# A two-layer hybrid decoder trunk: the last scaling as three tasks a row tile, four weight loads in halves, warm-up products on a constant

## The chip, the core and the metric

The kernel runs on one core of a Trainium2 chip. The metric is the device time of one execution in microseconds (us). All tensors in memory are float32. Five engines take part, each with its own instruction stream: TensorE (PE in the profile, with PEld for its weight loads), VectorE (DVE), ScalarE (ACT), GpSimd (POOL) and SyncE (SP), which issues nearly all transfers.

## What is computed

Each of two layers takes the residual stream x (256 rows of 1024), norms it, projects it to 3584 columns, lets three groups of heads attend, gates each group's output with a silu, and projects the 1024 gated columns back into x. A final norm with its own gain follows. Shortened:

```python
def reference(x, mem, norm_g, w_in, mem_norm_g, w_mem_kv, w_out, final_norm_g):
    for layer in range(2):
        h = rms_norm(x, norm_g[layer])
        proj = h @ w_in[layer]                     # 1024 -> 3584
        sb_q, sb_k, sb_v, sb_g, mb_q, mb_k, mb_v, mb_g, mem_q, mem_g = split(proj)
        o_sb = stick_breaking_attention(sb_q, sb_k, sb_v) * silu(sb_g)     # 6 heads of 64
        o_mb = moba_attention(rotary(mb_q), rotary(mb_k), mb_v) * silu(mb_g)  # 6 heads
        mk, mv = split(rms_norm(mem, mem_norm_g[layer]) @ w_mem_kv[layer])
        o_mem = memory_attention(mem_q, mk, mv) * silu(mem_g)              # 4 heads
        x = x + concat([o_sb, o_mb, o_mem]) @ w_out[layer]
    return rms_norm(x, final_norm_g)
```

## The kernel before, in words

**Order.** The program is recorded by a small scheduler (`Sched`). Tasks are Python generators; each yields the engine that it wants next and the names that must be ready, and the scheduler, with a cost for every operation, picks the task that can start first. What it picks is the fixed order of instructions on each engine. The costs do not run on the chip; there only the order and the semaphores count.

**Precision.** Every weight chunk `raw` comes by a transfer, is rounded to a high part by a cast (`hi_task`, the CAST `hl<-raw`, L290 on ACT or L311 on DVE) and gets a low part by a subtraction on DVE (`lo_task`, TENSOR_TENSOR `hl<-raw,hl`, L296). The activations have a high and a low part too, in `T`, and a product takes three terms. All products are recorded by the helper `mm` (L273).

**Weights.** The two layers' weights are cut into 107 chunks of 192 to 768 KB, in the order in which PE uses them (`chunks`). They share one ring of memory, `raw`: `dma_room` issues chunk j on SP once the scheduler has seen the low parts of all the chunks that lay in its place. `dma_chunk` issues one transfer a chunk (helper `dma`, L378). SP is one queue in program order, so a load that waits there holds up every later one. On the same queue go the attention weights' trips through memory: DVE transposes 32 by 32 blocks into `D`, SP stores `D` to `Z` (L1005) and loads it back rearranged into `T` or `F` (L1018, four loads a trip). PE then multiplies these by the values (`bank<-T,mv`, `bank<-T,mb_v`, `bank<-F,sb_v`).

Of the chunks that the change touches, chunk 38 is the last of the projection to sb_v in layer 0, chunk 52 the second of `w_out` in layer 0 (512 KB), chunk 68 the last of mb_k in layer 1 (192 KB), chunk 78 the first of sb_k in layer 1. Chunks 38 and 78 have 384 KB.

**Start.** `main` first fills a tile `junk` with zeros on DVE (L1131) and multiplies it with itself 14 times on PE (seven products of 512 columns, seven of 128), whose results nobody reads. The first real products are those of chunk 0 with the first 128 rows of the transposed x, which ACT and DVE scale into `T`.

**End.** In layer 1 the output projection gives, for each row tile t of 128 rows, the sums of two or three blocks of columns: 512 and 512 for t = 0, and 512, 256 and 256 for t = 1, of which the last starts from x in the accumulator. `resid_task` adds the block to x on DVE and squares it on ACT with a running sum. `gain_task` multiplies by the final gain `gb` on DVE. When the last block of a row tile is squared, `out_task` makes the reciprocal root with two small ACT instructions, scales the row tile by it in three pieces (columns 640 to 1023 on ACT, 0 to 255 and 256 to 639 on DVE) and stores each piece. In this version the three pieces are steps of one generator: the piece on ACT comes first and the next one is asked for only when it is recorded.

Of the kernel before, what the change touches and what calls it, by code (L numbers as in the profile page):

```python
# [9 lines left out]
BF = mybir.dt.bfloat16  # L10
# [6 lines left out]
D = 1024  # L17
# [45 lines left out]
ML_W = 0.0  # L63
ML_T = 300.0
ML_S = 200.0
MEM_AT = 0
ORDER = (["sb_qk", "mb_k", "mem_q", "mb_q", "mk", "mb_v", "mv", "sb_v", "sb_g", "mb_g", "mem_g"], ["mk",
         "mb_k", "mb_q", "mem_q", "sb_q", "sb_k", "mv", "mb_v", "mem_g", "mb_g", "sb_v", "sb_g"])
# [45 lines left out]
class Sched:  # L114
# [37 lines left out]
    def _avail(self, k, eng):  # L152
        r = k.req
        t = k.t
        if k.eng == eng:
            t += 0.0 if eng == "pe" else LAT_SAME
        elif k.eng:
            t += LAT_CROSS
        for n in r.get("need", ()):
            if n not in self.ready:  # L160
                return None
            t = max(t, self.ready[n])
        for tag in r.get("alloc", ()):
            items = self.res[tag].items
            spare = r.get("spare", 0)
            if callable(spare):
                spare = spare()
            if "form" in r and r["form"] == self.form:
                spare = r.get("spare2", spare)
            if len(items) <= spare:  # L170
                return None
            t = max(t, self.res[tag].best()[0])
        cond = r.get("cond")
        if cond is not None and not cond():
            return None
        return t + r.get("late", PE_LATE) if eng == "pe" and k.gen.__name__ != "main" else t
# [60 lines left out]
def hybrid_trunk(ctx: ExitStack, tc: tile.TileContext, x, mem, norm_g, w_in, w_mem_kv, w_out,  # L237
                 final_norm_g, xT, memT, gcols, consts, out):
    nc = tc.nc
# [234 lines left out]
    def dma_chunk(now=0.0, q=None):  # L474
        j = prog["dma"]
        if j >= len(chunks):
            return
        p, kk, c, w = chunks[j]
        n = len(kk)
        dma(raws(j).rearrange("p (k c) -> p k c", c=w),  # L480
            p.src[:, kk[0]:kk[0] + n, c:c + w], ("raw", j), q, now)
        prog["dma"] += 1
        if j in X_AT:
            load_xT(X_AT[j], X_AT[j] + 1, now=now)
        for t, at in enumerate((X0_AT, X1_AT)):
            if j == at:
                dma(xs[:, t, :], x_r[:, t, :], ("x", t), now=now)
        if j == CST_AT:
            dma(cst, consts[:, 0:512], "cst", now=now)
            dma(S.res["w"].items[0][2][:, :256], consts[:, 512:768], "msk", now=now)  # L490
# [14 lines left out]
    def lo_task():  # L505
        for j, (p, kk, _, w) in enumerate(chunks):
# [1 line left out]
            tt(los(j), raws(j), his(j).bitcast(F32), OP.subtract)  # L508
            S.mark(("lo", j))
            prog["lo"] = j + 1  # L510
            dma_room(S.cur.t)

    def urgent(which):
        return lambda: -5 if prog[which] <= prog["cur"] + URG else 60
# [18 lines left out]
    load_xT(2, 3)  # L533
    dma_chunk()
    load_xT(3, 4)
    dma_room()

    def bcast_row(vec, name):
        nc.gpsimd.dma_start(gb, bass.AP(tensor=vec.tensor, offset=vec.offset, ap=[[0, 128], [1, D]]))
# [574 lines left out]
    def out_task(t, nb):  # L1114
        r = ss[1, t][:, 7:8]
        yield from rstd(ss[1, t], nb, r)
        edge = (0, 512, 768, 1024) if nb == 3 else (0, 512, 1024)
        for eng, a, b, q in (("act", 640, D, nc.scalar if t else nc.sync), ("dve", 0, 256, nc.sync), ("dve", 256, 640, nc.sync)):
            yield R(eng, need=[("gain", n, t) for n in range(nb) if edge[n] < b and edge[n + 1] > a])
            s = xs[:, t, a:b]  # L1120
            if eng == "act":
                act(s, s, AF.Copy, scale=r)
            else:
                ts(s, s, r)
            q.dma_start(out_r[:, t, a:b], s)


    def main():
        hT, mT = Ts
        yield R("dve")  # L1130
        nc.vector.memset(junk, 0.0)  # L1131
        S.op("dve", 150.0)
        _, (acc,) = yield R("pe", alloc=["bank"])
        for n in (512,) * 7 + (128,) * 7:
            mm(acc[:, :n], junk[:, :128], junk[:, :n], True, True)
        S.free("bank", acc)
        scale_task(uT, ("xT",), 0, hT, ("h", 0), P_H0)
        for t in range(2):
# [177 lines left out]
    S.spawn(setup(), 0)  # L1316
    S.spawn(hi_task(), urgent("hi"))
    S.spawn(lo_task(), urgent("lo"))
    S.spawn(main(), 100)
    S.run()  # L1320

# [44 lines left out]
```

## Time and profile before

| | |
|---|---|
| median of 3 runs | 265.92 us (265.19 to 267.18) |
| the profiled execution | 265.58 us, of which the span of instructions is 263.8 us |
| granted TensorE clock | 0.993 |
| PE busy | 256.1 us (97%), 1597 products |
| DVE, ACT busy | 225.0 us (85%), 190.2 us (72%) |
| transfers | 67.05 MB, 254 GB/s over the span |

The page has six parts: busy time by engine; the span in 40 slices; the transfer queues; the chain of work that ended last, followed back from the last instruction; the costliest groups of instructions; and the issues of transfers with the time to their landing. The trace can also be asked for a timeline (start and duration in us, engine, line, operation, output and inputs, how many were merged, and in brackets how long the engine sat idle before it and what released it), for the table of waits (who waited for what: total, times, longest), and for the busy shares in chosen stretches. The products' ends are modelled and overlap the next product's start, so PE's busy share says little by itself; what PE waited for says more.

### The profile page before, as it was taken

How to read it: one execution, taken by the hardware profiler on the slowest of the kernel's cores; microseconds unless marked ns; L12 is line 12 of the kernel's file. 1: busy time of each engine (PE TensorE's matmuls, PEld its weight loads, DVE VectorE, ACT ScalarE, POOL GpSimd, SP SyncE). 2: the span in 40 equal slices, each digit the busy share in tenths (PEclk: the TensorE clock that was granted, in tenths of full speed). 3: DMA queues.
4: the chain of work that ended last, by engine and by line, in shares of the span. 5: the costliest groups of instructions: out<-in, count | busy, mean ns of one | idle time of the engine just before them, and what ended most of it. 6: DMA issues, size and time to landing. Idle time of an engine off the chain costs nothing.

```text
span 263.8 us, 4793 instructions
## 1 busy us (share of the span) xinstructions
PE 256.1 (97%) x1597; PEld 227.6 (86%) x1597; DVE 225.0 (85%) x517; ACT 190.2 (72%) x393; POOL 6.1 (2%) x18
## 2 busy tenths in 40 slices
PE   8999999999999999999999999999999999999990
PEld 5889999998899987878899998888898899787880
DVE  3878999999899999989799586999999995978353
ACT  4789995999698795967665272966897899356133
POOL 1002000000100000000000000000000000000000
PEclk9999999999999999999999999999999999999997
DMA  7999998989979999978955939599878996961004
GB/s 202 359 395 357 390 361 264 317 295 283 373 209 315 314 299 253 267 244 274 308 172 201 352 95 243 212 264 320 263 211 216 330 279 229 254 233 53 0 0 159
DMA packets 49880, 67.05 MB, mean 254 GB/s; under 512 B 4224, under 2 KB 41472, under 8 KB 49856
## 3 DMA queue, kind: packets, MB, share of 16 engines
q1 hardware_dynamic: 48912, 64.85, 77.4%
q0 software_dynamic: 512, 1.31, 1.7%
q10 hardware_dynamic: 432, 0.59, 0.7%
q8 instruction: 12, 0.20, 0.4%
q14 instruction: 12, 0.10, 0.1%
HBM read 57.29 MB, written 9.44 MB: 253 GB/s over the span
## 4 chain that ended last, share of the span: by engine, by line
PE 87%; DMA 7%; ACT 1%; SPq 1%; DVE 1%; issue 0%; DVEq 0%; ACTq 0%
PE bank L273 86%; DMA T<-Z 3%; DMA raw<-in_w_out_dram 3%; DMA raw<-in_w_in_dram 2%; PE bank L279 1%; SPq L1018 1%; ACT hl L290 1%; ACT junk L292 1%; DVE xs L296 1%; SPq L378 0%; DVE xs L304 0%; ACT ss L292 0%; DVE T L300 0%; DVEq L1362 0%; DVE ss L628 0%
## 5 line engine op out<-in xcount | busy, mean ns | idle before, releaser
L296 DVE TENSOR_TENSOR hl<-raw,hl 128x768 fp32r<-128x768 f32 (+5 forms) x107 | 99.6, 947 | 7.9 <-ACT hl L290 6.0
L273 PE MATMUL bank<-T,hl 128*128 128x256 f32 (+1 forms) x646 | 106.1, 322 | 0.2 <-DVE T L300 0.2
L273 PEld LDWEIGHTS bank<-T,hl 128*128 128x128 f32 x646 | 92.6, 189 | 11.7 <-issue 1.8
L290 ACT CAST hl<-raw 128x768 fp32r<-128x768 f32 (+5 forms) x105 | 85.3, 841 | 17.0 <-DMA raw<-in_w_in_dram 6.4
L273 PE MATMUL bank<-hl,T 128*128 128x384 f32 (+1 forms) x448 | 79.6, 335 | 0.0
L273 PEld LDWEIGHTS bank<-hl,T 128*128 128x128 f32 x448 | 76.5, 188 | 2.2 <-issue 0.3
L273 PE MATMUL bank<-hl,mxhi 128*128 128x512 f32 (+1 forms) x144 | 41.2, 367 | 0.0
L273 PEld LDWEIGHTS bank<-hl,mxhi 128*128 128x128 f32 x144 | 26.1, 189 | 4.9 <-issue 0.4
L273 PE MATMUL bank<-hl,mxlo 128*128 128x512 f32 (+1 forms) x72 | 26.3, 366 | 0.0
L877 DVE STREAM_TRANSPOSE D<-w 128x384 f32<-128x384 f32 (+1 forms) x32 | 19.2, 602 | 3.2 <-ACT w L292 2.9
L292 ACT ACTIVATE junk<-xs 128x512 bf16<-128x512 f32 (+1 forms) x12 | 7.3, 610 | 13.6 <-DVE xs L296 13.1
L273 PEld LDWEIGHTS bank<-hl,mxlo 128*128 128x128 f32 x72 | 13.6, 189 | 2.2
L292 ACT ACTIVATE T<-uT,gc 128x256 fp32r<-128x256 f32 x24 | 11.4, 506 | 2.7 <-DMA uT<-xT_dram 2.7
L810 DVE TENSOR_TENSOR_SCAN a<-a,a 128x256 f32<-128x256 f32 (+1 forms) x24 | 12.8, 539 | 0.1
L292 ACT ACTIVATE a<-bank 128x384 f32<-128x384 f32 x24 | 11.3, 483 | 1.6 <-DVE a L810 0.9
L292 ACT ACTIVATE w<-w,st 128x128 f32<-128x128 f32 (+1 forms) x24 | 10.7, 448 | 2.3 <-DVE st L830 2.2
L292 ACT ACTIVATE a<-a 128x384 f32<-128x384 f32 x24 | 11.8, 522 | 0.2
L300 DVE SCALAR_TENSOR_TENSOR T<-uT,gc,T 128x256 fp32r<-128x256 f32 x24 | 11.4, 476 | 0.6 <-ACT T L292 0.6
L304 DVE TENSOR_SCALAR w<-w,st 128x256 f32<-128x256 f32 (+1 forms) x40 | 11.2, 323 | 0.2
L296 DVE TENSOR_TENSOR xs<-bank,xs 128x512 f32<-128x512 f32 (+1 forms) x8 | 5.3, 656 | 6.6 <-PE bank L273 6.5
L292 ACT ACTIVATE w<-bank,st 128x256 f32<-128x256 f32 x16 | 7.4, 488 | 4.1 <-DVE st L843 4.1
L290 ACT COPY gT<-bank 128x256 f32<-128x256 f32 x10 | 3.6, 372 | 7.7 <-PE bank L273 7.7
(106 smaller groups left out, 218.6 us busy)
## 6 DMA issues: line engine op xcount, KB each, us to landing
raw<-in_w_in_dram SPq DMA_DIRECT2D x39, 384.0 KB, 4.8
Z<-D SPq DMA_DIRECT2D x16, 384.0 KB, 5.0
raw<-in_w_out_dram SPq DMA_DIRECT2D x8, 512.0 KB, 6.0
raw<-in_w_in_dram SPq DMA_DIRECT2D x18, 192.0 KB, 4.0
raw<-in_w_in_dram SPq DMA_DIRECT2D x6, 576.0 KB, 5.7
raw<-in_w_in_dram SPq DMA_DIRECT2D x13, 256.0 KB, 4.9
raw<-in_w_mem_kv_dram SPq DMA_DIRECT2D x6, 512.0 KB, 6.2
raw<-in_w_out_dram SPq DMA_DIRECT2D x4, 768.0 KB, 6.4
```

The costliest lines, as they stand in the source:

```text
L273: nc.tensor.matmul(out, lhsT=lhsT, rhs=rhs, start=start, stop=stop, **kw)
L279: nc.tensor.transpose(out, in_, idt)
L290: nc.scalar.copy(out, in_)
L292: nc.scalar.activation(out, in_, func, **kw)
L296: nc.vector.tensor_tensor(out, a, b, op=op)
L300: nc.vector.scalar_tensor_tensor(out, a, s, b, op0=op0, op1=op1)
L304: nc.vector.tensor_scalar(out, a, s, None, op0=op)
L810: nc.vector.tensor_tensor_scan(a[:, r0:r1], a[:, r0:r1], u[:, r0:r1], 0.0, OP.add, OP.add)
L877: nc.vector.transpose(o, w[:, :n * 128].rearrange("p (m j r) -> p m j r", j=4, r=32))
L1018: nc.sync.dma_start(Fv[32 * j:32 * j + 32, i0:i1], Zv.rearrange("(i r) (j e) -> j r i e", i=4, j=4)[j, :, i0:i1])
```

## The change

Four edits:

- `out_task` now makes the reciprocal root, marks it ready, and starts three tasks of a new function, `store_task`, one for each piece. The pieces of a row tile can now be recorded in any order, each with its own store. The last piece of t = 1 on ACT still goes out on ACT's own queue, all others on SP.
- `dma_chunk` splits the transfer of the chunks in `SPLIT` (38, 52, 68, 78) in two: by rows of the weight where the chunk has several blocks of 128 rows, by columns for chunk 68, which has one. The cast of a split chunk is still one instruction, so it needs both halves.
- The 14 first products multiply a constant of ones that the preamble writes on POOL before any engine starts, read with a step of zero, in place of `junk`. The filling of `junk` goes; it stays as the place that the squares are written to.
- A task that would issue loads one by one (`load_task`, with `after` in the scheduler) is written down but not started, since `LOADS` is 20.

```diff
--- before.py
+++ after.py
@@ -63,6 +63,9 @@
 ML_W = 0.0
 ML_T = 300.0
 ML_S = 200.0
+SPLIT = (38, 52, 68, 78)
+LOADS = 20
+P_LD = 50
 MEM_AT = 0
 ORDER = (["sb_qk", "mb_k", "mem_q", "mb_q", "mk", "mb_v", "mv", "sb_v", "sb_g", "mb_g", "mem_g"], ["mk",
          "mb_k", "mb_q", "mem_q", "sb_q", "sb_k", "mv", "mb_v", "mem_g", "mb_g", "sb_v", "sb_g"])
@@ -156,7 +159,7 @@
             t += 0.0 if eng == "pe" else LAT_SAME
         elif k.eng:
             t += LAT_CROSS
-        for n in r.get("need", ()):
+        for n in (*r.get("need", ()), *r.get("after", ())):
             if n not in self.ready:
                 return None
             t = max(t, self.ready[n])
@@ -477,8 +480,13 @@
             return
         p, kk, c, w = chunks[j]
         n = len(kk)
-        dma(raws(j).rearrange("p (k c) -> p k c", c=w),
-            p.src[:, kk[0]:kk[0] + n, c:c + w], ("raw", j), q, now)
+        dst, src = raws(j).rearrange("p (k c) -> p k c", c=w), p.src[:, kk[0]:kk[0] + n, c:c + w]
+        if j in SPLIT:
+            m = n // 2
+            one, two = ((slice(0, m), slice(0, w)), (slice(m, n), slice(0, w))) if m else ((slice(0, 1), slice(0, w // 2)), (slice(0, 1), slice(w // 2, w)))
+            dma(dst[:, one[0], one[1]], src[:, one[0], one[1]], None, q, now)
+            dst, src = dst[:, two[0], two[1]], src[:, two[0], two[1]]
+        dma(dst, src, ("raw", j), q, now)
         prog["dma"] += 1
         if j in X_AT:
             load_xT(X_AT[j], X_AT[j] + 1, now=now)
@@ -508,7 +516,15 @@
             tt(los(j), raws(j), his(j).bitcast(F32), OP.subtract)
             S.mark(("lo", j))
             prog["lo"] = j + 1
-            dma_room(S.cur.t)
+            if LOADS >= 20:
+                dma_room(S.cur.t)
+
+    def load_task():
+        while prog["dma"] < len(chunks):
+            j = prog["dma"]
+            yield R("sp", need=[("lo", max(rawp[j][1]))] if rawp[j][1] else [],
+                    after=[("raw", j - LOADS)] if j >= LOADS else [])
+            dma_chunk(S.cur.t)
 
     def urgent(which):
         return lambda: -5 if prog[which] <= prog["cur"] + URG else 60
@@ -533,7 +549,8 @@
     load_xT(2, 3)
     dma_chunk()
     load_xT(3, 4)
-    dma_room()
+    if LOADS >= 20:
+        dma_room()
 
     def bcast_row(vec, name):
         nc.gpsimd.dma_start(gb, bass.AP(tensor=vec.tensor, offset=vec.offset, ap=[[0, 128], [1, D]]))
@@ -1114,25 +1131,28 @@
     def out_task(t, nb):
         r = ss[1, t][:, 7:8]
         yield from rstd(ss[1, t], nb, r)
+        S.mark(("rstd", t))
+        for eng, a, b in (("dve", 0, 256), ("dve", 256, 640), ("act", 640, D)):
+            S.spawn(store_task(t, nb, r, eng, a, b), a // 256)
+
+    def store_task(t, nb, r, eng, a, b):
         edge = (0, 512, 768, 1024) if nb == 3 else (0, 512, 1024)
-        for eng, a, b, q in (("act", 640, D, nc.scalar if t else nc.sync), ("dve", 0, 256, nc.sync), ("dve", 256, 640, nc.sync)):
-            yield R(eng, need=[("gain", n, t) for n in range(nb) if edge[n] < b and edge[n + 1] > a])
-            s = xs[:, t, a:b]
-            if eng == "act":
-                act(s, s, AF.Copy, scale=r)
-            else:
-                ts(s, s, r)
-            q.dma_start(out_r[:, t, a:b], s)
+        yield R(eng, need=[("rstd", t)] + [("gain", n, t) for n in range(nb) if edge[n] < b and edge[n + 1] > a])
+        s = xs[:, t, a:b]
+        if eng == "act":
+            act(s, s, AF.Copy, scale=r)
+        else:
+            ts(s, s, r)
+        (nc.scalar if t and eng == "act" else nc.sync).dma_start(out_r[:, t, a:b], s)
 
 
     def main():
         hT, mT = Ts
         yield R("dve")
-        nc.vector.memset(junk, 0.0)
         S.op("dve", 150.0)
         _, (acc,) = yield R("pe", alloc=["bank"])
         for n in (512,) * 7 + (128,) * 7:
-            mm(acc[:, :n], junk[:, :128], junk[:, :n], True, True)
+            mm(acc[:, :n], nc.const_aps.tensor(1.0, [128, 128], BF), nc.const_aps.tensor(1.0, [128, n], BF), True, True)
         S.free("bank", acc)
         scale_task(uT, ("xT",), 0, hT, ("h", 0), P_H0)
         for t in range(2):
@@ -1316,6 +1336,8 @@
     S.spawn(setup(), 0)
     S.spawn(hi_task(), urgent("hi"))
     S.spawn(lo_task(), urgent("lo"))
+    if LOADS < 20:
+        S.spawn(load_task(), P_LD)
     S.spawn(main(), 100)
     S.run()
 
```

On PE and ACT the program has the same instructions in the same order, apart from the operands of the 14 first products. On DVE the filling of `junk` is gone and the end is in another order. The end of DVE's stream before, where `xs` is the row tiles, `ss10` and `ss11` hold the sums and the reciprocal roots of t = 0 and t = 1, and TENSOR_SCALAR on `xs` is a piece of the last scaling:

```order
L296 TENSOR_TENSOR xs_64<-bank7_97,xs_64 128x256
L296 TENSOR_TENSOR xs_64<-xs_64,gb_71 128x512
L628 TENSOR_SCALAR ss11_135<-ss11_135 128x1
L296 TENSOR_TENSOR xs_64<-xs_64,gb_71 128x256
L304 TENSOR_SCALAR xs_64<-xs_64,ss10_134 128x256
L296 TENSOR_TENSOR xs_64<-bank4_94,gb_71 128x256
L304 TENSOR_SCALAR xs_64<-xs_64,ss10_134 128x384
L304 TENSOR_SCALAR xs_64<-xs_64,ss11_135 128x256
L304 TENSOR_SCALAR xs_64<-xs_64,ss11_135 128x384
```

And now:

```order
L299 TENSOR_TENSOR xs_64<-bank7_97,xs_64 128x256
L299 TENSOR_TENSOR xs_64<-xs_64,gb_71 128x512
L307 TENSOR_SCALAR xs_64<-xs_64,ss10_134 128x256
L307 TENSOR_SCALAR xs_64<-xs_64,ss10_134 128x384
L645 TENSOR_SCALAR ss11_135<-ss11_135 128x1
L299 TENSOR_TENSOR xs_64<-xs_64,gb_71 128x256
L299 TENSOR_TENSOR xs_64<-bank4_94,gb_71 128x256
L307 TENSOR_SCALAR xs_64<-xs_64,ss11_135 128x256
L307 TENSOR_SCALAR xs_64<-xs_64,ss11_135 128x384
```

Both pieces of t = 0 moved ahead of three operations of t = 1. On SP the five stores stood in the order 384 (ACT's piece), 256 and 384 of t = 0, 256 and 384 of t = 1, and stand now as 256, 384 and 384 (ACT's piece) of t = 0, then 256 and 384 of t = 1.

SP's stream around chunk 52, before (`T1`, `F1` are the places of attention weights, `Z` their place in memory, `raw` from `in_w_out` are chunks 51, 52, and one row further on 53):

```order
L378 DMA raw_88<-in_w_in_dram 128x2x256
L378 DMA raw_88<-in_w_out_dram 128x2x512 x2
L1018 DMA T1_74<-Z1_112 32x4x192 x4
L1005 DMA Z0_111<-D0_107 128x768
L1018 DMA T1_74<-Z2_113 32x4x192 x4
L378 DMA raw_88<-in_w_out_dram 128x2x512
L1005 DMA Z1_112<-D1_108 128x768
L1018 DMA F1_106<-Z0_111 32x4x192 x4
```

And now:

```order
L381 DMA raw_88<-in_w_in_dram 128x2x256
L381 DMA raw_88<-in_w_out_dram 128x2x512
L381 DMA raw_88<-in_w_out_dram 128x512 x2
L1035 DMA T1_74<-Z1_112 32x4x192 x4
L1022 DMA Z0_111<-D0_107 128x768
L381 DMA raw_88<-in_w_out_dram 128x2x512
L1035 DMA T1_74<-Z2_113 32x4x192 x4
L1022 DMA Z1_112<-D1_108 128x768
L1035 DMA F1_106<-Z0_111 32x4x192 x4
```

Chunk 52 is two rows of one block each, and chunk 53's load moved ahead of the four loads from `Z2`. At the other three split chunks one more row stands and nothing else moved.

## The prediction

> **What bounds the kernel now.** I read the table of waits of PE first, because its busy share of 97% rests on modelled ends.
>
> ```profile
> PE bank L273 <- DVE junk L1131: 1.2, 1, 1.2
> PE bank L273 <- DMA T<-Z: 0.3, 1, 0.3
> PE bank L273 <- DVE T L300: 0.2, 1, 0.2
> ```
>
> These are all the waits of PE: 1.7 us in three places, none for a weight chunk (`hl`). The same table for PE's own weight loads, which overlap its products, has one short one:
>
> ```profile
> PEld bank L273 <- DVE hl L296: 0.2, 1, 0.2
> ```
>
> So PE does not stand still for a cast, a low part or a load of weights. The chain of waits tells the same and gives the places.
>
> ```profile
> 2.12 4.43 DMA raw<-in_w_in_dram
> ...
> 7.38 88.75 PE bank L273 x593
> ...
> 98.08 6.77 DMA raw<-in_w_out_dram
> ...
> 106.69 7.95 DMA T<-Z
> ...
> 140.16 114.79 PE bank L273 x696
> ```
>
> So there are three parts: a head to 7.38 us, set by the arrival of a weight load; a body in which PE computes without a break but for the 0.3 us near 114.7 (a load of attention weights, `T<-Z`, that went out at 106.69 and landed 7.95 later); and a tail from 254.95 to 263.8, 8.85 us, in which the last blocks are added, normed, scaled and stored. A change pays only in the head, in the tail, or by that one wait. The body is PE's own work, which the change leaves as it is.
>
> **The change part by part. Warm-up products on the constant.** The timeline of the first microseconds:
>
> ```profile
> 0.87 0.27 DVE L1131 MEMSET junk<- 128x256 uint32 x1 [0.87 <-PEq L1350]
> 1.19 3.37 PE L273 MATMUL bank<-junk 128*128 128x512 bf16 x14 [1.19 <-DVE junk L1131]
> 4.01 0.51 ACT L292 ACTIVATE T<-uT,gc 128x256 fp32r<-128x256 f32 x1 [1.99 <-DMA uT<-xT_dram]
> 4.57 2.58 PE L273 MATMUL bank<-T,hl 128*128 128x256 f32 x18
> ```
>
> DVE, free after the preamble at 0.87, fills `junk` in 0.27, and PE starts at 1.19. Without that wait PE can start when DVE could, near 0.87: 0.32 earlier, and 0.27 of DVE go. Neither reaches the path: the first real products start at 4.57 when ACT's scaled block is there (4.01 + 0.51 = 4.52), which waits for a load of x, and the next after 7.15 wait again until 7.38 for DVE (the last row of PE's waits), behind the load of weights that ends at 2.12 + 4.43 = 6.55. The cover is thus 0.05 us at 4.57 and a load of weights at 7.38. I take 0. The bounds: below, a gain of 0.2, the wait at 7.38 if it were to go, which nothing here supports; above, the constant is read with a step of zero, an operand form that no product in this trace has. The 14 products take at most 3.37 now. They may end at 4.57 + 0.23 (what PE idles before 7.38) = 4.80 before they cost anything, so from 0.87 they may last 3.93, or 1.17 times as long. At twice the length they would end at 0.87 + 6.74 = 7.61, a loss of 2.8. I take the row itself (the same 14 products, same sizes) as the nearest, and keep the loss as a rival.
>
> **Halved loads.** What must be known is whether the cast of the chunk waits for its load. ACT's rows for chunks 38, 52 (with 53), 68 (with 66 and 67) and 78 (with 77 and 79):
>
> ```profile
> 58.88 0.83 ACT L290 CAST hl<-raw 128x768 fp32r<-128x768 f32 x1
> ...
> 96.16 2.00 ACT L290 CAST hl<-raw 128x1024 fp32r<-128x1024 f32 x2 [0.35 <-PE bank L273]
> ...
> 130.49 1.33 ACT L290 CAST hl<-raw 128x384 fp32r<-128x384 f32 x3
> ...
> 155.74 2.37 ACT L290 CAST hl<-raw 128x768 fp32r<-128x768 f32 x3
> ```
>
> Three have no idle time before them: ACT came from other work, and the chunk lay ready. The second idled 0.35, but for PE, which had to finish with the place in `hl`. A half that arrives sooner is therefore worth 0 at all four, even before one asks whether PE waits for the cast. What it costs is one more issue on SP each and whatever the queue loses by smaller transfers. From the page's issues:
>
> ```profile
> raw<-in_w_in_dram SPq DMA_DIRECT2D x39, 384.0 KB, 4.8
> raw<-in_w_in_dram SPq DMA_DIRECT2D x18, 192.0 KB, 4.0
> ```
>
> Half the bytes land 0.8 us sooner, not in half the time. If the halves follow each other without overlap, a split costs 2 × 4.0 − 4.8 = 3.2; if the second runs behind the first, it costs one issue. The timeline of SP around chunk 52 (the first row), and PE's row that uses the loads behind it:
>
> ```profile
> 85.92 0.37 SPq L378 DMA_DIRECT2D raw<-in_w_out_dram  x1
> 86.38 1.84 SPq L1018 DMA_DIRECT2D T<-Z  x4
> 88.32 0.38 SPq L1005 DMA_DIRECT2D Z<-D  x1
> 88.74 3.25 SPq L1018 DMA_DIRECT2D T<-Z  x4
> 92.10 0.39 SPq L378 DMA_DIRECT2D raw<-in_w_out_dram  x1
> ...
> 102.15 0.82 PE L273 MATMUL bank<-T,mb_v 128*64 128x256 f32 x8
> ```
>
> An issue is 1.84 / 4 = 0.46. The loads `T<-Z` at 88.74 now stand behind chunk 53's load, which stood at 92.10, so they may go up to 0.46 + 0.39 later, and land behind 512 KB more; PE uses them at 102.15, more than 10 us after the last went out. The load on which PE waits at 114.7 went out at 106.69, some 14 us behind these, and the chain goes back from it to a load of weights issued at 98.08, not to SP's queue between 86 and 92, so an issue more there is swallowed before. I take 0 for all four splits, with a loss of 3.2 and a gain of 0.3 (the wait at 114.7 gone, because chunk 53's load is out of the way sooner) as ends. The Trainium skill, "DMA: Bandwidth & Descriptors", section "Rules for kernel authors", speaks against this edit: many small transfers should be joined into one large one, and below 64 KB one pays mostly overhead. The halves here have 96 to 256 KB; by the rows above the overhead is there too (0.8 for half the bytes), and the sum by the rule would be a loss somewhere below 3.2, by the rows' cover 0.
>
> **The last scaling.** DVE's and ACT's timelines of the tail:
>
> ```profile
> 256.75 0.68 DVE L296 TENSOR_TENSOR xs<-xs,gb 128x512 f32<-128x512 f32 x1
> 257.48 0.21 DVE L628 TENSOR_SCALAR ss<-ss 128x1 f32<-128x1 f32 x1
> 257.61 0.42 DVE L296 TENSOR_TENSOR xs<-xs,gb 128x256 f32<-128x256 f32 x1
> 257.94 0.35 DVE L304 TENSOR_SCALAR xs<-xs,ss 128x256 f32<-128x256 f32 x1
> 258.54 0.42 DVE L296 TENSOR_TENSOR xs<-bank,gb 128x256 f32<-128x256 f32 x1 [0.25 <-ACT junk L292]
> 258.88 1.00 DVE L304 TENSOR_SCALAR xs<-xs,ss 128x384 f32<-128x384 f32 x3
> ```
>
> ```profile
> 256.52 0.53 ACT L292 ACTIVATE ss<-ss 128x1 f32<-128x1 f32 x2
> ...
> 257.52 0.62 ACT L292 ACTIVATE xs<-xs,ss 128x384 f32<-128x384 f32 x1
> ...
> 258.54 0.53 ACT L292 ACTIVATE ss<-ss 128x1 f32<-128x1 f32 x2
> 259.10 0.61 ACT L292 ACTIVATE xs<-xs,ss 128x384 f32<-128x384 f32 x1
> ```
>
> The root of t = 0 is there at 257.05. The pieces of t = 0 now follow the gain at 256.75, which hands over near 257.34 (an operation starts some 0.09 before the last one's end: 257.61 + 0.42 against 257.94). The 256 columns take until 257.69; the 384 start a third of the three-piece row's 1.00 later, at 257.67, and end near 258.05. Then comes the sum of t = 1 (257.61 − 257.48 = 0.13 until the next starts), at 258.0 in place of 257.48; ACT needs it at 258.54, so 0.3 of cover is left. Then the gain (257.94 − 257.61 = 0.33), done by 258.5. The next gain starts at 258.54 as before, since it waits for ACT, and ends at 258.96. The root of t = 1 is there at 259.07. Before, the 384 columns of t = 0 stood in between, and the last piece ended at 259.88. Now the last two start at 259.10 and, with two thirds of 1.00, end at 259.77: 0.1 sooner. The stores:
>
> ```profile
> 258.17 2.50 SPq L1125 DMA_DIRECT2D out_dram<-xs  x5
> ...
> 260.21 0.46 SPq L1125 DMA_DIRECT2D out_dram<-xs  x1
> ```
>
> ```profile
> 259.74 0.37 ACTq L1125 DMA_DIRECT2D out_dram<-xs  x1
> ```
>
> ```profile
> 259.00:260.00 1.00, 0.00 (x0) 0.00 (x0) 0.88 (x3) 0.68 (x2) 0.00 (x0) 0.93 0.93 326
> ...
> 261.00:262.00 1.00, 0.00 (x0) 0.00 (x0) 0.00 (x0) 0.00 (x0) 0.00 (x0) 0.50 0.99 357
> ```
>
> Five stores leave SP from 258.17 to 260.21; the last column of the stretches is GB/s and the one before it the queues' busy share. SP's issues are 0.46 apart when they queue, so the last store went out at 260.21, 0.33 after its piece was done, and the one before it at 259.75: SP had been held by the stores of t = 0, whose last piece came from DVE after 258.88. Now t = 0 goes out at 257.72 (its first piece), 258.18 and 258.64 (ACT's piece is done at 258.14), then SP is idle until the first piece of t = 1 is done at 259.10 + 0.35 = 259.45, and the last store leaves at 259.48 + 0.46 = 259.94: 0.27 sooner. The other end: the 1 MB moves at 326 to 357 GB/s without a gap from 259 on, so the finish may follow the bytes. Then the 0.5 MB of t = 0, out 0.45 sooner (257.72 for 258.17) and with no piece held back to 259, are clear before t = 1 comes, whose bytes no longer queue behind them; at most the whole 0.45 goes through to the end. Between 0.27 and 0.45 I take 0.4, nearer to the bytes, since the queues are 0.99 busy just before the end.
>
> **Sum.** 0 + 0 − 0.4 on the profiled execution: 265.58 − 0.40 = 265.18. The median of the runs shown lies 0.34 above that execution, which would make it 265.52. I forecast 265.3, between the two: 0.2% faster, far within the 1% that a measurement of this kernel can tell from no change.
>
> **Rivals.** (1) The stores are bound at the end by landing alone and the new order gains nothing: 265.6. For it: the last store's queue share of 0.99. Against it: its bytes wait behind others that now go sooner. (2) The wait at 114.7 goes too: 265.18 − 0.3 = 264.9. For it: chunk 53's load leaves up to 3.4 us earlier (88.74 for 92.10) and clears the queue. Against: the chain goes back to a load issued at 98.08, which waits for DVE. (3) Slower: the split of chunk 52 and the load moved behind it make the attention weights for the products near 114.7 late. PE already waits there, so every bit counts from the first. The price is between 0.46 (one issue) and 3.2 (a serial half); the middle, 1.8, gives 265.18 + 1.8 = 267.0, the end 268.4. Against it: 14 us lie between. (4) Slower: the products on the constant take longer, from 1.17 times on; at twice the time 265.18 + 2.8 = 268.0. For it: no row shows that form. Against it: only the address step differs.
>
> **How the numbers follow.** The forecast 0.60, rival 1 0.13, rival 2 0.12, rival 3 0.10, rival 4 0.05. Faster by over 1% would be below 263.3, and no case reaches it: 0.03 for what I do not see. Slower by over 1% is above 268.6: rival 4 from a little over twice the time on, or rival 3's end of 268.4 with the scatter of the runs, together 0.06. The rest, 0.91, is no change. The range: down to 264.3, which is rival 2 less the 0.7 by which the lowest run lies under the median, rounded in; up to 267.0, rival 3's middle, which also covers the highest run, 267.18, less the 0.4.
>
> **What would show it.** Right: PE's waits keep `T<-Z` and `T` and lose `junk`; the first products start near 0.9 and the real ones still at 4.6 and 7.4; SP's last store leaves 0.87 after the second root's end (259.07 here) in place of 1.14; ACT's casts of the four chunks have no idle time for a load. Wrong: a first group of products that lasts over 3.9 us, a wait of PE for `T<-Z` over 0.5, or a row of waits with `hl`.

## The result and the profile after

The changed kernel takes 264.96 us (median of 9 executions, 264.51 to 265.07), the kernel before, run beside it, 266.33 (9 executions, 265.19 to 267.18 without one of 286.4, which the ratio leaves out). The ratio is 0.9949, with a 95% interval from 0.9929 to 0.9968. The forecast was 265.3 and no change that can be told; the time lies in its range and under 1%, but the gain is 1.4 us by the medians, and 1.07 by the profiled executions (265.58 and 264.51), where 0.4 was worked out. So the question is where the rest came from.

The waits of PE in the changed kernel, its weight loads left out, are a single row, the one before its first product (PEq is PE's sequencer):

```profile
PE bank L276 <- PEq L1372: 0.8, 1, 0.8
```

Both waits that the forecast kept are gone, the 0.2 for `T` at 7.38 and the 0.3 for `T<-Z` near 114.7. The head in the timeline of PE:

```profile
0.78 3.89 PE L276 MATMUL bank<-const-bfloat16-1.0 128*128 128x512 bf16 x14 [0.78 <-PEq L1372]
4.65 4.58 PE L276 MATMUL bank<-T,hl 128*128 128x256 f32 x27
```

The products on the constant start 0.41 sooner than those on `junk`, take 3.89 in place of 3.37, and the real ones start at 4.65 and run on without a break. The tail on DVE and on ACT:

```profile
256.30 0.68 DVE L299 TENSOR_TENSOR xs<-xs,gb 128x512 f32<-128x512 f32 x1
256.90 0.68 DVE L307 TENSOR_SCALAR xs<-xs,ss 128x256 f32<-128x256 f32 x2
257.49 0.21 DVE L645 TENSOR_SCALAR ss<-ss 128x1 f32<-128x1 f32 x1
257.62 0.42 DVE L299 TENSOR_TENSOR xs<-xs,gb 128x256 f32<-128x256 f32 x1
258.08 0.42 DVE L299 TENSOR_TENSOR xs<-bank,gb 128x256 f32<-128x256 f32 x1
258.65 0.68 DVE L307 TENSOR_SCALAR xs<-xs,ss 128x256 f32<-128x256 f32 x2
```

```profile
258.08 0.53 ACT L295 ACTIVATE ss<-ss 128x1 f32<-128x1 f32 x2
258.65 0.61 ACT L295 ACTIVATE xs<-xs,ss 128x384 f32<-128x384 f32 x1
259.29 0.35 ACTq L1146 DMA_DIRECT2D out_dram<-xs  x1
```

Both pieces of t = 0 are now scaled right behind their gain, and the last row stands alone: both pieces of t = 1 follow its root at once. SP's stores run from 257.27, and its last one leaves at 259.45, 0.84 behind the root's end (258.08 + 0.53):

```profile
257.27 2.60 SPq L1146 DMA_DIRECT2D out_dram<-xs  x5
```

```profile
259.45 0.42 SPq L1146 DMA_DIRECT2D out_dram<-xs  x1
```

**Where the 1.07 lies.** I compared the two executions product by product. Both have the same 1597 products, and between two waits they keep step to about 0.03 us, so the difference changes only at a few places. The start of PE's products is 0.17 ahead after 7.4, 0.48 after 114.8, and 0.45 at the last one. The two steps stand where the kernel before waited, at 7.38 and near 114.7. From the start of the last product to the landing of the last store it was 5.14 and is 4.76 (0.38 less), and from that landing to the end of the span it was 1.13 and is 0.89 (0.24 less). In sum 1.08. The last of these was in no reckoning of mine. It is a list on SP. A semaphore is a counter that a transfer raises when it has landed; the program closes with eight checks, one for each semaphore that the transfers use, in a fixed order and some 0.06 us apart in the trace. The transfers take these eight semaphores in turn, so the number of transfers decides where in the list the last store stands. Before, four more checks came after the one that waited for it; with four transfers more, it is the last of the list.

### The profile page after: what moved, and what is told of

The parts are those of the page before. It is cut to its first block, busy times and chain, and to the rows that moved or that the text cites. A ratio compares the mean times of both kernels' runs of the same rounds, so it can differ in the third digit from the quotient of the medians.

```text
span 262.7 us, 4802 instructions
## 1 busy us (share of the span) xinstructions
PE 256.6 (98%) x1597; PEld 228.0 (87%) x1597; DVE 224.6 (85%) x516; ACT 189.9 (72%) x393; POOL 6.1 (2%) x18
## 3 DMA queue, kind: packets, MB, share of 16 engines
q0 software_dynamic: 512, 1.31, 1.8%
## 4 chain that ended last, share of the span: by engine, by line
PE 97%; ACT 1%; DVE 0%; issue 0%; DVEq 0%; ACTq 0%
PE bank L276 96%; PE bank L282 1%; ACT junk L295 1%; ACT ss L295 0%; DVE xs L299 0%; DVE xs L307 0%; ACT xs L295 0%; DVEq L1384 0%; ACTq L295 0%
```

## The experiments

Each was timed in five rounds, the kernel before run beside it on the same chip. The theory at the start (A) was a sum of three parts, each taken as the work of the change: 0.4 from the stores, 0.3 from the wait at 114.7, 0.25 from the list. The rivals laid the gain on one edit, or on chance. Of the first four, three each take one part of the change to the kernel before, and the fourth halves other chunks.

**w_only, the warm-up products alone.**

```diff
-        nc.vector.memset(junk, 0.0)
...
-            mm(acc[:, :n], junk[:, :128], junk[:, :n], True, True)
+            mm(acc[:, :n], nc.const_aps.tensor(1.0, [128, 128], BF), nc.const_aps.tensor(1.0, [128, n], BF), True, True)
```

> The kernel before with the constant warm-up products alone (no memset, nothing else moved). Theory A (the gain is a sum of three: about 0.4 from the stores, 0.3 from the wait for T<-Z near 114.7 that went, 0.25 from the list of semaphore checks that SP works off after the last landing): no change, within 0.3 of the kernel before; first product near 0.8, the first real one still at 4.6, and PE's wait for T<-Z near 114.7, the 4 checks after the last landing and the store order as before. Rival B (the warm-ups carry the rest, by an earlier start or a steadier clock at the head): 0.5 to 0.9 faster, with PE ahead of the kernel before by that much before 20 us, and runs that scatter less.

Measured: 265.74 us against 265.74, ratio 1.0001 (0.9984 to 1.0018). PE's waits:

```profile
PE bank L273 <- PEq L1349: 0.8, 1, 0.8
PE bank L273 <- ACT hl L290: 0.5, 1, 0.5
```

No change in time, as theory A and the forecast have it, and the runs scatter as before (265.35 to 267.25): rival B falls. But theory A wanted the wait for `T<-Z` to be there, and it is not. Nothing that this kernel edits comes near 114.7. The row behind the first, a wait for a cast that ends at 9.9 us, is new.

**s_only, the last scaling alone.**

```diff
-        for eng, a, b, q in (("act", 640, D, nc.scalar if t else nc.sync), ("dve", 0, 256, nc.sync), ("dve", 256, 640, nc.sync)):
...
+        for eng, a, b in (("dve", 0, 256), ("dve", 256, 640), ("act", 640, D)):
+            S.spawn(store_task(t, nb, r, eng, a, b), a // 256)
```

> The kernel before with the last scaling in three tasks alone. Theory A: 0.4 faster, all of it behind PE's end: the last store leaves SP 2.1 after PE's end in place of 2.4 and lands 0.4 sooner counted from PE's end; 4 checks stand behind the last landing as before, so landing to end stays 1.13. Rival C (the stores carry everything, 1.1 to 1.4): 1.1 or more faster. Rival D (the landing of the bytes alone decides): 0 to 0.1 faster.

Measured: 265.35 us against 265.74, ratio 0.9988 (0.9965 to 1.0012). The interval holds no change too, but the profile is clear: from the last product to the last landing 4.78 us (5.14 before), from there to the end 1.13, as before. That is theory A's 0.4, and it rules out C, and D's 0 to 0.1 too. In this execution too PE waited for nothing but its start:

```profile
PE bank L273 <- DVE junk L1135: 1.2, 1, 1.2
```

**h_only, the four halved loads alone.**

```diff
+SPLIT = (38, 52, 68, 78)
...
+        if j in SPLIT:
...
+            dma(dst[:, one[0], one[1]], src[:, one[0], one[1]], None, q, now)
+            dst, src = dst[:, two[0], two[1]], src[:, two[0], two[1]]
+        dma(dst, src, ("raw", j), q, now)
```

> The kernel before with the four splits alone, chunk 53's load moved up with them. Theory A: 0.55 faster: 0.3 from PE's wait for T<-Z near 114.7 that is gone, and 0.25 behind the last landing, because four more transfers put the last store's semaphore at the end of SP's closing list (0 checks after it in place of 4; landing to end 0.87 in place of 1.13). Rival E (the wait near 114.7 is chance of one execution): 0.25 faster, with the wait there in some profiles and not in others. Rival F (neither; halves cost nothing and bring nothing, as predicted): within 0.1 of the kernel before.

Measured: 265.51 us against 265.74, ratio 0.9986 (0.9968 to 1.0005): 0.23, which is rival E's number by the medians; the interval holds A's 0.55 too, and no change. From the last product to the last landing 5.12, as before; from there to the end 0.90. No wait near 114.7. The head of this execution shows one source of the scatter:

```profile
1.19 3.91 PE L274 MATMUL bank<-junk 128*128 128x512 bf16 x14 [1.19 <-DVE junk L1137]
4.86 4.35 PE L274 MATMUL bank<-T,hl 128*128 128x256 f32 x23
```

The stretches of a microsecond on PE, with the products begun in each (x), here and then in s_only:

```profile
5.00:6.00 1.00, 1.00 (x6) 1.00 0.70 225
6.00:7.00 1.00, 1.00 (x7) 1.00 0.94 297
```

```profile
5.00:6.00 1.00, 1.00 (x6) 1.00 0.86 253
6.00:7.00 1.00, 1.00 (x11) 1.00 0.97 368
```

Products of 256 columns go at half rate (213 ns each) until 7.1 us in h_only and until 5.9 in s_only, and at 120 ns after; the column before the queues' share, the granted clock, reads 1.00 in all four rows. At 8.4 us h_only is 0.56 behind s_only, and it is 0.56 behind at its last product. The end of the half rate came between 3.9 us (the kernel before) and 7.1 over the profiles, whatever the kernel. The Trainium skill, "TensorE: Matmul & The Clock Gate", section "What's actually happening", tells of a free-running activity window of 3.4 us, so that the moment of full speed moves with where in it the first product falls, by 0.5 either way. A moment that moves fits; by these profiles it moves by 3.2 us.

**l4, four other chunks halved.** They were chosen so that no instruction and no load changes its place among the others; SP only issues four transfers more. The edit is h_only's with other numbers.

```diff
-SPLIT = (38, 52, 68, 78)
+SPLIT = (45, 48, 87, 90)
```

> The kernel before with four other chunks split (45, 48, 87, 90), so that no load or instruction changes its place among the others: SP only issues 4 transfers more. Theory A: 0.25 faster, all of it after the last landing (0 checks after it in place of 4; landing to end 0.87 in place of 1.13), with PE's wait for T<-Z near 114.7 as before (0.2 to 0.4). Rival E (that wait is chance): 0.25, and the wait may be gone. Rival F (the closing list costs nothing, the splits neither): within 0.1 of the kernel before.

Measured: 265.42 us against 265.74, ratio 0.9982 (0.9963 to 1.0000): 0.32. From the last landing to the end 0.89. So four halves of other chunks bring the same 0.24. PE has another wait in this execution, for `F<-Z` (0.2), and falls behind by another 0.5 near 108.

After these four, the wait at 114.7 was struck from the theory: two kernels that do not touch that place do not have it. What stayed is A': 0.37 from the stores and 0.24 from the list, 0.6 in all. The second four test this sum.

**a_again, the changed kernel once more, on the chip of the next three.**

> The changed kernel once more, against the kernel before on one chip. Theory A' (after the single edits: the stores give 0.37, the closing list 0.24, and the wait for T<-Z near 114.7 and the head were chance of one execution): 0.6 faster, the tail from the last product's start to the last landing 4.76 and from there to the end 0.89, no PE wait near 114.7. Rival G (the three edits together do more than the sum, 1.1 to 1.4, as the first measurement had it): 1.1 or more faster.

Measured: 264.69 us (264.48 to 264.73, 6 runs) against 266.12, ratio 0.9952 (0.9935 to 0.9969). The first measurement is confirmed and A' is too small: the gain is 1.3, not 0.6. The tail is as A' has it (4.75, then 0.89). Behind its start PE had one wait, which ended at 9.55 us:

```profile
PE bank L276 <- ACT hl L293: 0.3, 1, 0.3
```

**s_l4, the new last scaling and four other chunks halved.** It has both parts of A' and nothing else of the change.

```diff
+SPLIT = (45, 48, 87, 90)
...
+            S.spawn(store_task(t, nb, r, eng, a, b), a // 256)
```

> The kernel before with the last scaling in three tasks and four other chunks split (45, 48, 87, 90): no constant warm-ups, chunks 38, 52, 68, 78 whole, chunk 53's load in its old place. Theory A': 0.6 faster, as the changed kernel, within 0.15 of it. Rival H (chunk 52 and the earlier load of chunk 53, or the warm-ups, carry a part): 0.2 or more slower than the changed kernel.

Measured: 265.20 us (264.51 to 266.35) against 266.12, ratio 0.9962 (0.9941 to 0.9982). Its lowest runs are as low as the changed kernel's, its median is 0.5 above. That is rival H's "0.2 or more" and not the 0.15 of A', by the medians; the intervals of the two ratios overlap. The difference lies in the runs that are not at the lowest. The profile caught one (266.35):

```profile
PE bank L274 <- DVE junk L1141: 1.2, 1, 1.2
PE bank L274 <- ACT gT L293: 1.0, 1, 1.0
```

```profile
99.13 1.05 ACT L291 CAST hl<-raw 128x1024 fp32r<-128x1024 f32 x1 [2.04 <-DMA raw<-in_w_out_dram]
100.19 1.28 ACT L960 ACT_TABLE_LOAD   x1
101.49 0.84 ACT L293 ACTIVATE gT<-gT 128x768 f32<-128x768 f32 x1
```

The second fence is ACT's timeline: it waited 2.04 for chunk 53's load, and the gate `gT`, which PE needs, stands behind that cast. In the changed kernel the same place reads:

```profile
96.00 2.00 ACT L293 CAST hl<-raw 128x1024 fp32r<-128x1024 f32 x2 [0.38 <-PE bank L276]
98.01 1.28 ACT L971 ACT_TABLE_LOAD   x1
99.31 0.85 ACT L295 ACTIVATE gT<-gT 128x768 f32<-128x768 f32 x1
```

No wait for a load, and the gate 2.2 sooner. SP tells why, in s_l4 and in the changed kernel:

```profile
88.28 4.67 SPq L1024 DMA_DIRECT2D T<-Z  x4
93.06 0.39 SPq L379 DMA_DIRECT2D raw<-in_w_out_dram  x1
```

```profile
84.78 1.30 SPq L381 DMA_DIRECT2D raw<-in_w_out_dram  x2
86.17 1.80 SPq L1035 DMA_DIRECT2D T<-Z  x4
88.08 0.38 SPq L1022 DMA_DIRECT2D Z<-D  x1
89.44 0.40 SPq L381 DMA_DIRECT2D raw<-in_w_out_dram  x1
90.28 1.85 SPq L1035 DMA_DIRECT2D T<-Z  x4
```

In s_l4 four loads of `T<-Z` take 4.67, not four issues of 0.46. Transfer by transfer, the third of them goes out at 92.16. The whole chunk 52, eight transfers before it, landed at 92.15 (issued at 85.46, 6.7 to landing). Each semaphore serves every eighth transfer, so the program holds a transfer on SP until the one eight before it has landed: in all 14 profiles none that SP or ACT issued left sooner, and the closest left 0.015 behind. In the kernel before, the same hold ends at 91.22, when chunk 52 landed at 91.20. With chunk 52 in halves, these land at 90.27 and 90.86, and the two loads that wait for them go out at 90.28 and 90.88; chunk 53's load stands ahead of all four, at 89.44 and not at 92.1 to 93.7. It lands at 95.9 to 96.6 in all seven profiles with chunk 52 halved, and at 96.8 to 99.5 in the seven without. Two things changed there at once: the halves end the hold sooner, and the scheduler gave the load another place on SP. No run has one without the other. By an estimate from the changed kernel's rows most of it is the place: behind the four loads, chunk 53's would wait for the `T<-Z` load eight before it, which landed at 91.46, so it could not leave before that, 2.0 later than it does.

**a_sp0, the changed kernel with no splits.**

```diff
-SPLIT = (38, 52, 68, 78)
+SPLIT = ()
```

> The changed kernel without its splits (four transfers fewer). Theory A': 0.24 slower than the changed kernel, all of it behind the last landing (1.13 from there to the end in place of 0.89), so 0.37 faster than the kernel before. Rival H: slower than that by a wait of PE for T<-Z near 114.7 that comes back, 0.55 in all. Rival F (the closing list is nothing): the changed kernel's time.

Measured: 264.99 us (264.56 to 266.68), ratio to before 0.9977 (0.9958 to 0.9997), 0.30 above the changed kernel. From the last landing to the end 1.13, as A' has it; the 0.24 of the list and the 0.30 agree within the scatter. Rival F falls by the profile; by the times alone it would not, since the two intervals overlap.

**a5, a fifth chunk halved.**

```diff
-SPLIT = (38, 52, 68, 78)
+SPLIT = (38, 45, 52, 68, 78)
```

> The changed kernel with a fifth chunk split (45), one transfer more, nothing else moved. Theory A': the last store's semaphore is now the first of SP's closing list, so seven checks stand behind the last landing: 1.31 from there to the end in place of 0.89, 0.42 slower than the changed kernel, 0.2 faster than the kernel before. Rival F (the number of transfers is of no account): the changed kernel's time within 0.1. Rival I (each check more is put down to the splits' own cost): 0.06 slower or less.

Measured: 265.01 us (264.69 to 265.53, and one of 268.03), ratio to before 0.9975 (0.9952 to 0.9997): 0.32 above the changed kernel, 0.42 expected. One 192 KB half more, nothing else moved, and by the median it is slower. The span, and the stores of that execution:

```profile
core 0: 263.2 us, clock 0.995
```

```profile
259.53 0.40 SPq L1146 DMA_DIRECT2D out_dram<-xs  x1
```

The last store landed 2.37 later, at 261.90, and the end is 1.31 behind that, to the hundredth what seven more checks of 0.06 make. Over all kernels the stretch is 0.89 with no check behind the last landing, 1.08 with three, 1.13 with four, and 1.31 with seven. The checks themselves stand in these traces one behind the other, and the closing list is shown.

That left 0.65 of the 1.3 open. The changed kernel's 15 runs lie within 0.6 (264.48 to 265.07), those of the single edits spread over 1.4 to 2. Theory K took the halved chunk 52 and the earlier warm-ups to be what keeps the runs together, and undid each.

**a_junk, the changed kernel with the old warm-ups; a_no52, the changed kernel with chunk 90 halved in place of 52; w_h, the changed kernel with the old last scaling.** Their edits to the changed kernel, in this order:

```diff
+        nc.vector.memset(junk, 0.0)
...
-            mm(acc[:, :n], nc.const_aps.tensor(1.0, [128, 128], BF), nc.const_aps.tensor(1.0, [128, n], BF), True, True)
+            mm(acc[:, :n], junk[:, :128], junk[:, :n], True, True)
```

```diff
-SPLIT = (38, 52, 68, 78)
+SPLIT = (38, 68, 78, 90)
```

```diff
+        for eng, a, b, q in (("act", 640, D, nc.scalar if t else nc.sync), ("dve", 0, 256, nc.sync), ("dve", 256, 640, nc.sync)):
```

> The changed kernel with its warm-up products on the zeroed tile again: the new last scaling and the four splits stay. What is open: the changed kernel's 15 runs all lie within 0.6 (264.48 to 265.07), those of the single edits spread over 1.5 to 2, and its gain of 1.3 is 0.65 more than the 0.61 of stores and closing list. Theory K (two sources of spread: the head, where the clock is granted in full between 5.0 and 7.1 and the earlier constant warm-ups make a late grant rarer; and waits of PE between 101 and 117, which the profiles show in three of six kernels with chunk 52 whole and in none of five with it halved and chunk 53's load ahead): median 0.3 to 0.6 above the changed kernel, runs up to 266, no wait of PE between 101 and 117. Rival L (warm-ups are of no account): the changed kernel's times, 264.5 to 265.1.

> The changed kernel with chunk 90 split in place of chunk 52: as many transfers, chunk 52 whole and chunk 53's load back in its old place. Theory K: the lowest runs as the changed kernel's (264.5), the median 0.3 to 0.6 above it, with runs up to 266 that have waits of PE between 101 and 117. Rival M (which chunks are halved is of no account, only their number): the changed kernel's times, 264.5 to 265.1.

> The kernel before with the constant warm-ups and the four splits, and the old last scaling. Theory K: both sources of spread are gone, so the runs lie within 0.7, 0.37 above the changed kernel's: 264.85 to 265.5, median 265.2. Rival N (the new last scaling has a part in the spread): runs up to 266.5.

Measured, against 265.65 for the kernel before: a_junk 264.98 (264.47 to 266.23), ratio 0.9971 (0.9949 to 0.9993); a_no52 265.13 (264.33 to 267.00), ratio 0.9989 (0.9966 to 1.0012); w_h 265.16 (264.75 to 266.60), ratio 0.9981 (0.9962 to 0.9999). The medians of a_junk and a_no52 lie 0.29 and 0.44 above a_again's, where K put them, though a_junk's lies on the changed kernel's first one, and a_again ran on another chip (266.12 for the kernel before there, 265.65 here). But w_h has both of K's parts and a run of 266.60, where K allowed 265.5; and the wait of a_no52's profile is at the head, not between 101 and 117:

```profile
PE bank L276 <- PEq L1372: 0.8, 1, 0.8
PE bank L276 <- ACT T L295: 0.7, 1, 0.7
```

So K is at most half borne out, and that by medians whose intervals overlap. The last run took its stronger half by itself.

**only52, the kernel before with chunk 52 alone in halves.**

```diff
+SPLIT = (52,)
```

> The kernel before with chunk 52 alone in halves (chunk 53's load goes up with it), one transfer more. Theory O (SP's transfer number n goes out only when number n - 8 has landed, as the profiles show 13 times out of 13 at this place; with chunk 52 whole, a T<-Z load stands 0.4 to 3.4 us until it has landed at 91.2 to 92.8, and chunk 53's load behind it): chunk 53's load leaves SP near 89.4 in place of 92.1 to 93.7 and lands by 96.8 (97.9 to 99.5 in most profiles with chunk 52 whole), PE has no wait between 101 and 117; three checks stand behind the last landing, so 1.07 from there to the end; median 0.3 to 0.5 faster, 0.06 of it from the closing list. Rival P (the halves bring only what the closing list gives): 0.06 faster, and the highest quarter of the runs as high as before's.

Measured: 265.60 us (264.89 to 267.12) against 266.06, ratio 0.9983 (0.9961 to 1.0006). By the medians that is 0.46, as theory O has it; the interval holds rival P's 0.06 and no change, and the highest runs are as high as before's (267.12 and 267.23). SP behaves as O says, chunk 53's load leaves at 89.44 and lands at 95.97, and 1.08 lies behind the last landing. But PE waited after all:

```profile
PE bank L274 <- DVE junk L1137: 1.2, 1, 1.2
PE bank L274 <- DMA T<-Z: 0.9, 2, 0.6
```

```profile
114.93 1.08 PE L274 MATMUL bank<-T,mv 128*64 128x256 f32 x8 [0.58 <-DMA T<-Z]
...
116.97 1.08 PE L274 MATMUL bank<-T,mv 128*64 128x256 f32 x8 [0.30 <-DMA T<-Z]
```

The first is the wait of the kernel before (0.25 there), for the same load, the fourth of eight: it went out at 107.34 and landed at 114.79. The chain of waits of this execution leads to the second, through the load of a weight chunk:

```profile
104.56 8.35 DMA raw<-in_w_out_dram
112.91 0.02 issue
112.92 3.79 DMA T<-Z
116.72 0.25 issue
116.97 1.05 PE bank L274 x7
```

That eighth `T<-Z` load was held until the transfer eight before it, a chunk of `w_out` issued at 104.56, had landed at 112.91, 8.35 later. A long load of that chunk does not by itself make PE wait: in w_only, a_sp0 and the changed kernel it took 8.72, 8.71 and 8.54, and PE waited for nothing there. At the first place it is a race. The fourth load landed between 111.95 and 114.79 over the 14 profiles, and PE was ready for it between 114.03 and 115.81 (an estimate: the product before it, and the 0.32 between the two where PE does not wait). It came 0.19 late in the kernel before and 0.52 late in only52, but 0.15 ahead in the changed kernel and 0.4 to 2.6 ahead in the others. Theory O's claim that PE would not wait is wrong.

**Where PE loses time.** All 14 profiles have the same products in the same order, so they can be laid over each other. Against a_sp0, whose last product starts first, the others lose time in two stretches only. In the first 12 us they lose up to 1.06 (h_only). Between 100 and 118 us ten of the 14 lose nothing, and the kernel before loses 0.3, l4 0.9, only52 1.3 and s_l4 1.8. Everywhere else 12 of the 13 keep step with a_sp0 to 0.04, and s_l4 to 0.16. If the runs without a profile are like these, what is open of the 1.3 lies in these two stretches. Of the seven profiles with chunk 52 whole three lose time in the second one, of the seven with it halved one does. That is too few to show what the halves do.

**All runs in one fit.** I fitted the times of all kernels (least squares) with a term for the new scaling, one for each check behind the last landing, one for the constant, and one for chunk 52 in halves. Of 266 runs, six over 267.6 us are left out, five of the kernel before and one of a5. The terms, with 95% intervals from drawing the runs anew: new scaling −0.45 us (−0.63 to −0.28); one check 0.04 (0.01 to 0.08), so four of them −0.17; constant −0.12 (−0.31 to 0.05); chunk 52 −0.34 (−0.52 to −0.16). The sum, −1.08, is near the −1.3 measured. The kernels were timed in groups, and the kernel before differs between the groups (265.65 to 266.33); with a term for each group the four come out at −0.40, 0.04, −0.10 and −0.39. The fit takes the parts to add up, and one pair does not show its last term: h_only and l4, timed together, differ only in which chunks are halved and in chunk 53's place, and have 265.51 and 265.42, though 12 runs each, spread over 2.0 and 1.4, leave room for it.

## Why the prediction was right, and where it was short

**The warm-ups: 0, and 0 measured** (ratio 1.0001). The start was put at 0.87 and was 0.78. The 14 products took 3.89, just within the limit of 3.9, and rival 4's fear did not come: a product on the constant takes 427 ns at 512 columns, the same as one on `junk` before the rate rises. They took longer because the seven of 128 columns ran at half rate (107 ns), which ran at 56 ns in the kernel before's profiled execution, and the last one of 512 columns took 427 in place of 283; the old ones last as long in s_only and h_only (3.91). I had read 3.37 as the length of the group, and it was one draw. The real products at 4.65 were called. The waits of PE were not: the prediction kept `T` at 7.38 and `T<-Z` near 114.7, and both are gone in the changed kernel. The wait at 7.38 was not there in any later profile, so it too was a draw.

**The halves: 0 taken, about 0.2 to 0.5 by the medians.** This is the step that failed: "I take 0 for all four splits". Its argument on the casts holds, no cast waited for a half. But it asked only who waits for the split chunk and what its issue costs SP. Two things hang on a transfer beside these: its place in the turn of eight semaphores, which sets the closing list (0.24, shown by l4, a_sp0, a5 and only52), and the transfer eight behind it, which the program holds on SP until the first has landed. What the second is worth is not shown. That hold stood in my own quotation, as a row of four loads that took 3.25 us, and I read it as a place where an issue "is swallowed". Rival 2 had chunk 53's load leave up to 3.4 earlier, and it left 2.7 earlier (89.44 for 92.10), for the most part by its new place in the order.

**Rival 2's time, 264.9, is the one that came, but not by its way.** The wait at 114.7 went from the profile. It is also missing in w_only and s_only, where nothing near it changed, and came back, larger, in only52, where chunk 53's load was out of the way as the rival wanted it. Of 14 profiles two have it. What rival 2 named, the earlier load of chunk 53, is real. For a worth of it speak the fit (0.34) and one stall seen without it (s_l4); h_only beside l4 does not show it. That the rival's time came is thus in part luck. Rival 3, the same edit as a loss, has nothing for it. The Trainium skill, "DMA: Bandwidth & Descriptors", section "Rules for kernel authors", would join small transfers into a large one. For these halves of 96 to 256 KB the runs show no loss: h_only is 0.23 faster by its median, and its interval holds no change.

**The last scaling: 0.4 taken, 0.38 in the profile of after, 0.36 in s_only, 0.45 (0.28 to 0.63) in the fit.** The steps came out one by one: the last store was to leave 0.87 after the root's end and left 0.84 after it; the first store was to go 0.45 sooner and, counted from the last product's start, went 0.44 sooner (0.20 for 0.64). Taking a value near the upper bound came out, and rival 1 falls. The forecast of no change over 1% came out because this term was right and those put at nothing are small. The mechanism was right for this 0.4 and for the 0 of the warm-ups; the rest of the 1.3 was not foreseen.

**The base.** The forecast stood 0.3 under the 265.58 of the profile and within the scatter of three runs. The kernel before's medians were 266.33 beside the changed kernel and 265.65, 265.74, 266.06 and 266.12 on the chips of the experiments, so the first 265.92 was a fair one; its execution in the profile was a lower draw.

**Open.** Why the changed kernel's 15 runs hold together so closely, when w_h, a_sp0, a_junk and a_no52, each one edit away, reach 266.2 to 267.0, is not settled. Of those four kernels' 48 runs 12 lie above 265.5; if each run had that chance of one in four, 15 in a row below it would be a draw of about one in 75, so chance alone is unlikely but not excluded. Three sources of scatter were seen (the moment of full rate, the first loads, the loads near 100 to 117), but no single edit was shown to remove one. So of the 1.3, about 0.6 is shown (0.38 from the stores, 0.24 from the list), and the rest, about 0.65, is not; the fit lays 0.3 of it on chunk 52.

## What to carry to other kernels

Ask of a transfer not only who reads it, but what the queue holds until it has landed, and what the count of transfers does to the program's end: here four transfers more gave 0.24 us at the end, and a fifth took 0.42 there (0.32 by the medians). Do not budget a wait of 0.3 us from one profile; two kernels that left its cause alone lost it. When the last stores fill the queues, scale and send the first row tile's pieces as soon as they are ready, and count the gain from the first store's time, not only from the last one's.

## What was unexpected of the hardware

- In this program transfer number n waits for the landing of number n − 8, counted over SP's and ACT's (92.16 behind 92.15 in s_l4; 90.28 and 90.88 behind 90.27 and 90.86 in the changed kernel). A large transfer can so stop SP at the eighth after it: two issues around such a hold were up to 3.65 us apart (s_only, the later at 111.50) where an issue takes 0.46.
- The closing list costs 0.06 us for each check that stands after the one that waits for the last landing: 0.89, 1.08, 1.13 and 1.31 us to the end with 0, 3, 4 and 7 of them.
- The rate of the first products doubles between 3.9 and 7.1 us after the span's start, from one execution to the next, while the granted-clock column reads 1.00 throughout (0 to 8 us in all 14 profiles).
